# A decoder layer on one core: a tile of their own for the memory's raw weights, and VectorE alone for the low parts of the mixer's value weights

## The chip, the cores and the metric

The kernel runs on one core of a Trainium2 chip. The time is device microseconds of one execution, and a kernel's time is the median of its runs. Five engines work beside each other: TensorE (PE; its weight loads are listed as PEld), VectorE (DVE), ScalarE (ACT), GpSimd (POOL) and SyncE (SP). Here SP does nothing but issue transfers, and POOL issues some too. Each engine takes its instructions strictly in the order in which they were put on it.

## What is computed

One layer, for 512 tokens of a prompt and 64 tokens of samples (576 together), all in float32:

```
u    = rms(x) * g_pre_mix;   proj = u @ w_in            # z, xbc, dt, q, k, v, gates
y_ssd = rms(ssd_scan(...) * silu(z)) * g_ssm_out
h_ml  = rms(mlstm_scan(q, k, v, ...)) * g_mlstm_out * sigmoid(og)
x = x + rms(concat(y_ssd, h_ml) @ w_out) * g_post_mix   # the output projection
mk, mv = (rms(mem) * g_mem) @ w_mem_k,  ... @ w_mem_v   # 256 rows of memory, 4 heads
x = x + rms(cross_attention(rms(x) * g_pre_x, mk, mv) @ w_xo) * g_post_x
x = x + rms(swiglu(rms(x) * g_pre_ffn)) * g_post_ffn
```

What matters below are two of these products: `v`, the mixer's values (part of `u @ w_in`), and the output projection with the preparation of the memory's weights for head 3 beside it.

## The kernel before

Every large product is taken in three matmuls on numbers that are split into a high part (rounded to the matmul's type) and a low part (what is left): high by high, high by low, low by high (L201 to L203; L772 to L774 for the values). Weights come in units of 128 x 1024 numbers, 512 KB. `split_w` (L173) does this for one unit: SP loads it into a `raw` tile (two buffers), ACT rounds it into `whi` (L181), and a low part `wlo` is made from `raw` and `whi` (three buffers each). The next load into a `raw` buffer waits until its last reader is done, and the next `whi` waits until PE has finished with the unit three before it.

The low part is made in one of three ways. `cut` says how many of the 1024 columns VectorE subtracts (L188). For the other columns, with `acc=True`, ACT writes the negated high part into `wlo` (L185), and POOL issues a transfer that adds the raw weights to it from memory (L186); without `acc`, GpSimd subtracts. The mixer's projection (the `win` tiles) and the values (`wv`, eight units, two for each of four heads) use `cut` 512 with `acc=True`.

The values are computed by `gemm_tok` (L753) around 165 to 250 us, in between the chunks of the SSD scan (tiles `lm`, `ps_yi`, `xs`, `h`) and other projections. A scheduler that simulates a timeline sets the order of instructions on every engine, so that these pieces are woven into each other.

The output projection, about 401 to 512 us, runs in two passes over eight output tiles j. The first (`ps_o1`) takes the SSD half. The second (`out2`, L1139, `ps_o2`) takes the mLSTM half; its units are called o0 to o7 here. Each output tile has two halves of tokens, the first of 256 and the second of 320. For j = 0 to 3 the second half and then the first are done together; for j = 4 to 7 first all second halves, then the first halves of 7, 6, 5 and 4, the unit o4 being loaded a second time. Beside each `out2(j)` of j = 0 to 3 stand `presplit` (parts of later weights: loaded by POOL, rounded by ACT into `preh`, subtracted by VectorE and written back by POOL), `memory` (the memory's activations: squares on ACT, sums on VectorE) and `wm_split(j)`.

`wm_split` (L1153) makes the high and low parts of four weight units of the memory's head 3, whole, into `wmh` and `wml`, by `split_w` with `to=`: so the load goes through the same two `raw` buffers as the units of the output projection, ACT rounds (L192) and VectorE subtracts (L193). `wmh` takes the place of `mixs_h`, which the first pass reads to its end. PE first needs `wmh` and `wml` after the output projection, from 512.6 us.

Of the kernel before, what the change touches and what calls it, by code (L numbers as in the profile page):

```python
# [11 lines left out]
F32 = mybir.dt.float32  # L12
# [3 lines left out]
ALU = mybir.AluOpType  # L16
# [3 lines left out]
P = 128  # L20
# [88 lines left out]
CUT = 512  # L109
# [7 lines left out]
def build(nc, tc, ctx, I, O):  # L117
    V, A, G, S, TE = nc.vector, nc.scalar, nc.gpsimd, nc.sync, nc.tensor
# [17 lines left out]
    def GP(name="g"):  # L136
        return pg.tile([P, 512], F32, name=name, tag="g")
# [33 lines left out]
    loads = []  # L171

    def split_w(src, n=1024, cut=CUT, acc=False, pool=None, to=None, raw=None):  # L173
        if raw is None:
            raw = wp.tile([P, 1024], F32, name="raw", tag="raw", bufs=2)
        loads.append(S.dma_start(raw[:, :n], src))
        if to:
            split(*to, raw[:, :n])
            return to
        hi, lo = [(pool or wp).tile([P, 1024], F32R, name=k, tag=k, bufs=NWX if pool else 3) for k in ("whi", "wlo")]  # L180
        A.copy(hi[:, :n], raw[:, :n])  # L181
        for e, a, b in ((V, 0, cut), (G, cut, n)):
            if b > a and e is G and acc:

                A.activation(lo[:, a:b], hi[:, a:b].bitcast(F32), AF.Copy, scale=-1.0)  # L185
                G.dma_start(lo[:, a:b], src[:, a:b], accum_op=ALU.add)  # L186
            elif b > a:
                e.tensor_tensor(lo[:, a:b], raw[:, a:b], hi[:, a:b].bitcast(F32), op=ALU.subtract)  # L188
        return hi, lo

    def split(hi, lo, src, eng=None):
        A.copy(hi, src)  # L192
        (eng or V).tensor_tensor(lo, src, hi.bitcast(F32), op=ALU.subtract)  # L193
# [12 lines left out]
    def gemm2(units, xh, xl, evac, name, halves=(0, 1), alloc=None, order=None, parts=HALVES):  # L206
        for i in halves:
            t0, n = parts[i]
            ps = (alloc or GP)(name)[:, :n]
            m = gemm(ps, units, xh, xl, t0, n, order=order)  # L210
            evac(t0, n, ps)
        return m

    def act(t):
        return lambda k, t0, n: t[:, k, t0:t0 + n]
# [455 lines left out]
    for g in range(2):  # L671
        for hb in range(2):
            dst = cpad[:, g, 4 * hb:4 * hb + 4, :].rearrange("p b t -> p (b t)")
            src = bc[:, 2 + g, TP + 32 * hb:TP + 32 * hb + 32]
# [4 lines left out]
    for g in range(2):  # L679
# [13 lines left out]
        for h in range(8):  # L693
            k, j = h % 2, (8 * g + h) // 2
# [55 lines left out]
        G.memset(v_[:, :, 256:257], 1.0)  # L750
        G.memset(v_[:, :, 257:258], 0.0)

    def gemm_tok(src, xh_, xl_, chunks, evac, acc=False, units=None):  # L753

        units = units or [split_w(src[:, i, :], acc=acc) for i in range(2)]
        for c0 in range(0, len(chunks), 2):
            ps = GP("ps_v")
            for c, (t0, n) in enumerate(chunks[c0:c0 + 2]):
                if n == TS:

                    for k in range(KT):
                        hi, lo = units[k // 4]
                        j = (k % 4) * 256
                        mm(ps[:, 0:256], xh_(k, t0, P), hi[:, j:j + 256], start=k == 0, stop=k == KT - 1, skip_group_check=True)
                        mm(ps[:n, 0:256], xh_(k, t0, n), lo[:, j:j + 256], start=False, stop=k == KT - 1, skip_group_check=True)
                    break
                for k in range(KT):
                    hi, lo = units[k // 4]
                    j = (k % 4) * 256
                    ah, al = xh_(k, t0, n), xl_(k, t0, n)  # L770
                    o = ps[:n, c * 256:c * 256 + 256]
                    mm(o, ah, hi[:, j:j + 256], start=k == 0, stop=False, skip_group_check=True)  # L772
                    mm(o, al, hi[:, j:j + 256], start=False, stop=False, skip_group_check=True)
                    m = mm(o, ah, lo[:, j:j + 256], start=False, stop=k == KT - 1, skip_group_check=True)  # L774
            evac(c0, ps)
        return m
# [12 lines left out]
    for h in range(4):  # L789
        gemm_tok(I["wv"][h], U, UL, CHUNKS, v_evac(h), True)  # L790
# [29 lines left out]
    for h in range(4):  # L820
# [17 lines left out]
        for c in range(4):  # L838
# [3 lines left out]
                        op=ALU.mult)  # L842
# [233 lines left out]
    at = st.enter_context(tc.tile_pool(name="attn", bufs=1, reuse_waits="tile"))  # L1076
# [6 lines left out]
    evs, ahead = [], []  # L1083
# [43 lines left out]
    def memory_norm():  # L1127
        rmem[0] = rstd_cols([ssqm], CHUNKS[:2], "rmem", alloc=B1)
        rstd_rows(rmem[0], CHUNKS[:2], rmem_b, B1)
# [9 lines left out]
    def out2(j, i):  # L1139
        return gemm2([(*weights(("o", j), I["wout"][j, 1], cut=1024), KT)], act(mixm_h), act(mixm_l), o2_evac(j), "ps_o2", [i])  # L1140
# [9 lines left out]
    wmh, wml = SL0("wmh").rearrange("p k t -> p (k t)"), SL(2, "wml", F32R).rearrange("p k t -> p (k t)")  # L1150
    wm = [(wmh[:, 1024 * i:1024 * i + 1024], wml[:, 1024 * i:1024 * i + 1024]) for i in range(4)]

    def wm_split(i):  # L1153
        split_w(I["wmk"][6 + i] if i < 2 else I["wmv"][3][:, i - 2, :], to=wm[i])

    def chain2(i, js):

# [4 lines left out]

    for j in range(4):
        out2(j, 1)
        out2(j, 0)
        presplit(j < 3)
        memory(range(2 * j, 2 * j + 2))
        wm_split(j)
    memory_norm()
    for j in range(4, 8):  # L1170
        out2(j, 1)
# [171 lines left out]
    mk, m = mem_key(3, wm[:2])  # L1343
# [29 lines left out]
    for h in range(3, -1, -1):  # L1373
        xq(2 * h + 1, 0)
        xq(2 * h, 0)
        if last:
            mk = mem_key(h)
# [219 lines left out]
    for n_, (key, p) in enumerate(order):  # L1597
        src = I[{"xo": "wxo", "g": "wgate", "u": "wup"}[key[0]]][key[1]]
# [813 lines left out]
```

## Time and profile before

| What | Value |
|---|---|
| runs (3) | 1118.76 us median, 1115.33 to 1123.21 |
| the profiled execution | 1119.24 us, its span 1117.5 us |
| granted TensorE clock, mean | 0.997 |
| PE busy | 1095.2 us (98%) |
| PE busy, first 16 us / last 18 us of the span | 13.84 us / 10.92 us |
| DVE, ACT, POOL busy | 770.2, 609.5, 225.2 us |
| moved by DMA | 184.44 MB, mean 165 GB/s |

The profile of one execution lists for each instruction its start, its length and, where its engine stood idle before it, what ended that idle time. "PE ps_o L201 <- ACT whi L181: 3.8, 2, 2.0" reads: PE, before writing the tile `ps_o` at line 201, waited for ACT's instruction on `whi` at line 181, 3.8 us in total, 2 times, 2.0 us at most. The view of stages gives for a stretch of time each engine's busy time, the granted clock (1.00 is full), the share of time that the 16 DMA engines were busy, and GB/s. In the timelines a row is start, length, engine, line, operation, written and read tiles, shapes and count.

### The profile page before, as it was taken

To read this page: it belongs to the slowest core of one execution; us is meant where nothing else is said; L and a number is where in the kernel's file an instruction comes from. 1 tells how busy PE (TensorE), PEld (TensorE's weight loads), DVE (VectorE), ACT (ScalarE), POOL (GpSimd) and SP (SyncE) were. 2 spreads that over 40 slices of the span, in tenths; PEclk is the share of its full clock that TensorE was granted. 3 is DMA by queue.
4 is the path that set the end of the run, shared out by engine and by line. 5 is a ranking of instruction groups with operands and counts; after the bars stand their busy time and mean duration, and the time that the engine had idled before them with its cause. 6 is when DMAs were issued, how large, how long until landed. Compare 5 with 4: busy or idle time off the path is not lost.

```text
span 1117.5 us, 21277 instructions
## 1 busy us (share of the span) xinstructions
PE 1095.2 (98%) x8355; PEld 1043.7 (93%) x8355; DVE 770.2 (69%) x1521; ACT 609.5 (55%) x1130; POOL 225.2 (20%) x309
## 2 busy tenths in 40 slices
PE   9999999999999999989999999999999999999997
PEld 8999889798998999989988889999999999999997
DVE  6796775457786785558755455686578878887655
ACT  6867534355563465556534445644465556556654
POOL 1343544323122121110044301100000210020000
PEclk9999999999999999989999999999999999999999
DMA  6785565634564437863487765742552873397432
GB/s 209 171 152 131 132 179 145 177 86 143 143 192 125 122 141 264 279 229 95 152 257 263 250 212 164 233 152 94 165 157 86 186 168 90 83 234 218 101 139 85
DMA packets 60584, 184.44 MB, mean 165 GB/s; under 512 B 6684, under 2 KB 10908, under 8 KB 59972
## 3 DMA queue, kind: packets, MB, share of 16 engines
q1 hardware_dynamic: 44324, 142.19, 39.0%
q0 software_dynamic: 15872, 40.38, 17.1%
q8 instruction: 65, 1.06, 0.4%
q10 hardware_dynamic: 288, 0.52, 0.1%
q14 instruction: 35, 0.29, 0.1%
HBM read 153.75 MB, written 29.30 MB: 164 GB/s over the span
## 4 chain that ended last, share of the span: by engine, by line
PE 82%; DVE 4%; DMA 4%; ACT 3%; issue 2%; DVEq 0%; ACTq 0%; SPq 0%; POOLq 0%
PE ps_in L201 5%; PE ps_in L203 5%; PE ps_in L202 5%; PE ps_g L1725 3%; PE ps_g L1726 3%; PE ps_g L1727 3%; PE ps_u L1726 2%; PE ps_u L1725 2%; PE ps_u L1727 2%; PE ps_o L201 2%; PE ps_o L203 2%; PE ps_o L202 2%; PE ps_dn L201 2%; PE ps_dn L203 2%; PE ps_dn L1932 2%; PE ps_dn L202 2%
## 5 line engine op out<-in xcount | busy, mean ns | idle before, releaser
L201 PE MATMUL ps_in<-uh,whi 128*128 128x320 f32 (+1 forms) x544 | 165.4, 304 | 1.3 <-DVE cb L426 1.1
L203 PE MATMUL ps_in<-uh,wlo 128*128 128x320 f32 (+1 forms) x544 | 163.1, 300 | 0.0
L202 PE MATMUL ps_in<-ul,whi 128*128 128x320 f32 (+1 forms) x544 | 162.2, 298 | 0.0
L181 ACT CAST whi<-raw 128x1024 fp32r<-128x1024 f32 (+1 forms) x102 | 102.9, 1011 | 79.5 <-PE ps_in L202 20.1
L188 DVE TENSOR_TENSOR wlo<-raw,whi 128x512 fp32r<-128x512 f32 (+1 forms) x94 | 86.2, 917 | 60.3 <-ACT whi L181 59.6
L201 PEld LDWEIGHTS ps_in<-uh,whi 128*128 128x128 f32 x544 | 103.0, 189 | 3.9 <-DVE cb L426 1.4
L203 PEld LDWEIGHTS ps_in<-uh,wlo 128*128 128x128 f32 x544 | 102.9, 189 | 1.7 <-issue 1.3
L202 PEld LDWEIGHTS ps_in<-ul,whi 128*128 128x128 f32 x544 | 103.1, 189 | 0.8
L186 POOL DMA_DIRECT2D wlo<-win x32 | 28.3, 884 | 93.6 <-ACT wlo L185 83.3
L1725 PE MATMUL ps_g<-b,whi 128*128 128x288 f32 x144 | 42.7, 297 | 1.2 <-ACT cc L1793 1.0
L201 PE MATMUL ps_o<-mixm_h,whi 128*128 128x256 f32 (+1 forms) x128 | 39.4, 308 | 3.8 <-ACT whi L181 3.8
L1725 PE MATMUL ps_u<-b,whi 128*128 128x288 f32 x144 | 42.8, 297 | 0.0
L1726 PE MATMUL ps_u<-b,whi 128*128 128x288 f32 x144 | 42.5, 295 | 0.0
L1726 PE MATMUL ps_g<-b,whi 128*128 128x288 f32 x144 | 42.5, 295 | 0.0
L202 PE MATMUL ps_o<-mixm_l,whi 128*128 128x256 f32 (+1 forms) x128 | 39.0, 305 | 0.0
L203 PE MATMUL ps_o<-mixm_h,wlo 128*128 128x256 f32 (+1 forms) x128 | 38.7, 306 | 0.0
L201 PE MATMUL ps_xo<-qh,whi 128*128 128x288 f32 x128 | 38.0, 302 | 0.4 <-ACT whi L181 0.3
L201 PE MATMUL ps_xq<-u2h,whi 128*128 128x320 f32 (+1 forms) x128 | 38.2, 303 | 0.0
L202 PE MATMUL ps_xq<-u2l,whi 128*128 128x320 f32 (+1 forms) x128 | 38.0, 298 | 0.0
L203 PE MATMUL ps_xq<-u2h,wlo 128*128 128x320 f32 (+1 forms) x128 | 37.9, 296 | 0.0
L202 PE MATMUL ps_xo<-ql,whi 128*128 128x288 f32 x128 | 37.7, 295 | 0.0
L774 PE MATMUL ps_v<-wlo,uh 128*128 128x256 f32 x128 | 36.7, 290 | 0.9 <-DMA wlo<-wv 0.9
(777 smaller groups left out, 3914.4 us busy)
## 6 DMA issues: line engine op xcount, KB each, us to landing
raw<-win SPq DMA_DIRECT2D x35, 512.0 KB, 3.7
raw<-wout SPq DMA_DIRECT2D x17, 512.0 KB, 4.5
kva<-kc SPq DMA_DIRECT2D x16, 512.0 KB, 7.0
kva<-vc SPq DMA_DIRECT2D x16, 512.0 KB, 7.0
raw<-wxq SPq DMA_DIRECT2D x13, 512.0 KB, 3.7
raw<-wgate SPq DMA_DIRECT2D x13, 512.0 KB, 5.3
raw<-wup SPq DMA_DIRECT2D x13, 512.0 KB, 4.3
wlo<-win POOLq DMA_DIRECT2D x24, 256.0 KB, 5.4
```

The source lines that it names most:

```text
L181: A.copy(hi[:, :n], raw[:, :n])
L186: G.dma_start(lo[:, a:b], src[:, a:b], accum_op=ALU.add)
L188: e.tensor_tensor(lo[:, a:b], raw[:, a:b], hi[:, a:b].bitcast(F32), op=ALU.subtract)
L201: mm(ps, wh, ah, start=i == 0, stop=False)
L202: mm(ps, wh, al, start=False, stop=False)
L203: m = mm(ps, wl, ah, start=False, stop=i == len(tiles) - 1)
L774: m = mm(o, ah, lo[:, j:j + 256], start=False, stop=k == KT - 1, skip_group_check=True)
L1725: mm(ps, wh, b[0][:, k, :], start=start and k == 0, stop=False, skip_group_check=True)
L1726: mm(ps, wh, b[1][:, k, :], start=False, stop=False, skip_group_check=True)
L1727: m = mm(ps, wl, b[0][:, k, :], start=False, stop=k == 3, skip_group_check=True)
L1932: mm(ps, wh, bl, start=False, stop=False, skip_group_check=True)
```

## The change

The first part touches `gemm_tok`. Where it splits its own units, the parameter `acc` now selects `cut`: the values, which pass `True`, get `cut=1024`, so VectorE subtracts all 1024 columns and neither L185 nor L186 is called; the memory's values pass nothing, get `cut=CUT` (512) and stay as they were. The `win` tiles keep their adding transfers.

The second part replaces `wm_split` by two functions. `wm_load(j)` loads the memory's unit into a tile `wmr` of its own. This tile has one buffer, in the place of `mk`, which is written only later. The load is issued behind the latest `raw` load, and `wm_load` stands between the second and the first half of `out2(j)`. `wm_split(j)` then rounds on ACT, behind the latest evacuation of the output projection, and subtracts on VectorE.

```diff
-    def gemm_tok(src, xh_, xl_, chunks, evac, acc=False, units=None):
+    def gemm_tok(src, xh_, xl_, chunks, evac, acc=None, units=None):
 
-        units = units or [split_w(src[:, i, :], acc=acc) for i in range(2)]
+        units = units or [split_w(src[:, i, :], cut=CUT if acc is None else 1024) for i in range(2)]
...
-    def wm_split(i):
-        split_w(I["wmk"][6 + i] if i < 2 else I["wmv"][3][:, i - 2, :], to=wm[i])
+    def wm_load(i):
+        t_ = at.tile([P, 1024], F32, name="wmr", tag="mk", bufs=1)
+        with tc.issue_after(loads[-1].ins):
+            S.dma_start(t_, I["wmk"][6 + i] if i < 2 else I["wmv"][3][:, i - 2, :])
+        return t_
+
+    def wm_split(i, t_):
+        hi, lo = wm[i]
+        with tc.issue_after(evs[-1].ins):
+            A.copy(hi, t_)
+        V.tensor_tensor(lo, t_, hi.bitcast(F32), op=ALU.subtract)
...
     for j in range(4):
         out2(j, 1)
+        wm_raw = wm_load(j)
         out2(j, 0)
         presplit(j < 3)
         memory(range(2 * j, 2 * j + 2))
-        wm_split(j)
+        wm_split(j, wm_raw)
```

The scheduler moves instructions of other lines too, between about 140 us and 500 us. Three places matter for the steps below.

SP's queue in the second pass of the output projection, before. The rows named `wout` are the units o1 to o7, in order; `wmk` and `wmv` are the memory's units 0 to 3.

```order
L176 DMA raw_5520<-wmk 128x1024
L176 DMA raw_5524<-wout 128x1024
L176 DMA raw_5606<-wmk 128x1024
L176 DMA raw_5610<-wout 128x1024
L176 DMA raw_5692<-wmv 128x1024
L176 DMA raw_5696<-wout 128x1024
L176 DMA raw_5776<-wmv 128x1024
L176 DMA raw_5796<-wout 128x1024
L176 DMA raw_5832<-wout 128x1024
L176 DMA raw_5868<-wout 128x1024
L176 DMA raw_5904<-wout 128x1024
```

And after, where o1 to o7 are the seven `wout` rows from `raw_5508` to `raw_5888`:

```order
L1156 DMA wmr_5462<-wmk 128x1024
L176 DMA raw_5508<-wout 128x1024
L176 DMA raw_5594<-wout 128x1024
L176 DMA raw_5680<-wout 128x1024
L176 DMA raw_5780<-wout 128x1024
L176 DMA raw_5816<-wout 128x1024
L1156 DMA wmr_5544<-wmk 128x1024
L176 DMA raw_5852<-wout 128x1024
L1156 DMA wmr_5630<-wmv 128x1024
L176 DMA raw_5888<-wout 128x1024
L1156 DMA wmr_5716<-wmv 128x1024
```

Five units of the output projection now follow each other, and the memory's units 1 to 3 come later, each between two of them.

ACT's queue in the same place, before: the rounding of the memory's unit 3, and then those of o4 (`whi_5798`) and o5 (`whi_5834`).

```order
L192 CAST wmh_5442<-raw_5776 128x1024
L266 ACTIVATE sq_5642<-f_mix_4903 128x320
L1136 ACTIVATE f_mix_4903<-f_mix_4903,par_77 128x320
L266 ACTIVATE sq_5672<-f_mix_4903 128x256
L266 ACTIVATE sq_5684<-memraw_4909 128x256
L1136 ACTIVATE f_mix_4903<-f_mix_4903,par_77 128x256
L1091 CAST preh_5676<-prel_5594 128x1024
L181 CAST whi_5798<-raw_5796 128x1024
L266 ACTIVATE sq_5689<-memraw_4909 128x256
L181 CAST whi_5834<-raw_5832 128x1024
```

And after: the memory's units 2 (`wmr_5630`) and 3 (`wmr_5716`), with o6 (`whi_5854`) and o7 (`whi_5890`).

```order
L1162 CAST wmh_5426<-wmr_5630 128x1024
L266 ACTIVATE sq_5675<-memraw_4893 128x256
L266 ACTIVATE sq_5712<-f_mix_4887 128x320
L1136 ACTIVATE f_mix_4887<-f_mix_4887,par_77 128x320
L181 CAST whi_5854<-raw_5852 128x1024
L266 ACTIVATE sq_5744<-f_mix_4887 128x256
L266 ACTIVATE sq_5754<-memraw_4893 128x256
L1136 ACTIVATE f_mix_4887<-f_mix_4887,par_77 128x256
L1091 CAST preh_5748<-prel_5666 128x512
L266 ACTIVATE sq_5759<-memraw_4893 128x256
L1162 CAST wmh_5426<-wmr_5716 128x1024
L181 CAST whi_5890<-raw_5888 128x1024
```

o4 stood behind the memory's last unit before; now o4 stands ahead of the memory's unit 1, o6 behind its unit 2, and o7 right behind its unit 3.

POOL's queue while the values are computed, as a difference (`h` and `xs` belong to the SSD scan):

```order
 L722 TENSOR_TENSOR h_1896<-h_1896,decs 128x1024
-L631 TENSOR_TENSOR xs<-xs,ec 128x384
-L186 DMA wlo<-wv 128x512
-L631 TENSOR_TENSOR xs<-xs,ec 128x384
-L186 DMA wlo<-wv 128x512
+L631 TENSOR_TENSOR xs<-xs,ec 128x384 x2
 L722 TENSOR_TENSOR h_1925<-h_1925,decs 128x1024
 L722 TENSOR_TENSOR h_1924<-h_1924,decs 128x1024
-L186 DMA wlo<-wv 128x512
```

The adding transfers of the values are gone from POOL, here three of the eight; the subtractions that replace them are rows of VectorE that grow from 512 to 1024 columns.

## The prediction, made before the result was known

> **What bounds the kernel now.** I read the page first, then what PE waited for, then the stages around its longest wait, then PE's own timeline there, then the chain that ended last.
>
> ```profile
> span 1117.5 us, 21277 instructions
> PE 1095.2 (98%) x8355; PEld 1043.7 (93%) x8355; DVE 770.2 (69%) x1521; ACT 609.5 (55%) x1130; POOL 225.2 (20%) x309
> ...
> PE ps_o L201 <- ACT whi L181: 3.8, 2, 2.0
> PE ps_nh L911 <- DMA c<-c: 1.7, 1, 1.7
> PE ps_hs L715 <- DMA h<-h: 1.5, 1, 1.5
> ...
> PE ps_v L774 <- DMA wlo<-wv: 0.9, 2, 0.7
> ```
>
> PE is the bound: it is idle for only 22.3 of 1117.5 us. The edit removes no PE work, so it can earn only idle time, and time at a low granted clock. The largest wait of all (3.8 us) is at the output projection for a unit's high part. Two smaller ones, `ps_hs` and `ps_v`, stand where the values are computed.
>
> ```profile
> 470.00:474.00 4.00, 4.00 (x33) 4.00 (x32) 0.95 (x1) 0.00 (x0) 0.00 (x0) 1.00 0.95 335
> 474.00:478.00 4.00, 4.00 (x33) 4.00 (x32) 2.21 (x4) 2.69 (x6) 1.08 (x2) 1.00 0.33 90
> 478.00:481.00 3.00, 0.89 (x5) 0.42 (x3) 2.52 (x5) 2.62 (x5) 0.09 (x1) 1.00 0.88 295
> 481.00:484.00 3.00, 1.27 (x5) 1.27 (x6) 2.71 (x5) 2.31 (x5) 0.46 (x1) 0.62 0.66 210
> 484.00:487.00 3.00, 3.00 (x13) 3.00 (x13) 1.70 (x4) 2.67 (x5) 0.54 (x1) 0.50 0.91 313
> 487.00:490.00 3.00, 3.00 (x18) 3.00 (x17) 0.83 (x3) 0.25 (x1) 0.00 (x0) 0.74 0.88 261
> ```
>
> Columns: stretch, its length, busy time of PE, PEld, DVE, ACT, POOL, granted clock, DMA share, GB/s. PE falls to 0.89 of 3 us, and then the clock falls to half: the hole goes on costing while PE is "busy" again.
>
> ```profile
> 474.06 0.31 PE L203 MATMUL ps_o<-mixm_h,wlo 128*128 128x320 f32 x1
> 475.23 0.31 PE L202 MATMUL ps_o<-mixm_l,whi 128*128 128x320 f32 x1
> ...
> 477.92 0.28 PE L202 MATMUL ps_o<-mixm_l,whi 128*128 128x256 f32 x1
> 478.04 0.28 PE L203 MATMUL ps_o<-mixm_h,wlo 128*128 128x256 f32 x1
> 480.36 0.42 PE L201 MATMUL ps_o<-mixm_h,whi 128*128 128x320 f32 x1 [2.03 <-ACT whi L181]
> ...
> 482.73 0.63 PE L201 MATMUL ps_o<-mixm_h,whi 128*128 128x320 f32 x1 [1.81 <-ACT whi L181]
> ...
> 490.00 0.31 PE L201 MATMUL ps_o<-mixm_h,whi 128*128 128x320 f32 x1
> ```
>
> At full clock eight 320-column matmuls are 1.17 us, so 0.146 each, and a 256-column one is 0.12. Unit o4 was due at 478.16. From 480.36 to 490.00 PE issues 34 matmuls, 34 x 0.146 = 5.0 us of work in 490.00 - 478.16 = 11.84. **The hole costs 6.8 us**: 3.8 of waiting, 3.0 of low clock.
>
> ```profile
> 458.10 4.70 DMA raw<-wmv
> ...
> 465.47 8.73 DMA raw<-wmv
> 474.23 1.06 ACT wmh L192
> 475.31 1.24 DVE wml L193
> 476.56 4.99 DMA raw<-wout
> 481.63 1.05 ACT whi L181
> 482.73 0.63 PE ps_o L201
> ```
>
> The chain says why: the load of the memory's unit 3 took 8.73 us in one of two `raw` buffers. ACT and VectorE had to use it up before o5 could be loaded into that buffer, at 476.56. Between 474 and 478 the transfers were nearly idle (0.33, 90 GB/s) while weights were wanted: a buffer was missing, not bandwidth.
>
> **Part 1, a tile for the raw memory weights.** Loads, roundings and subtractions stay four each. What goes is the turn in `raw`: o1 to o5 load one behind another, each when the unit two before it is split. o4 is rounded when PE leaves o1 (465.4 by the 6.4 us of 24 x 0.146 + 24 x 0.12), o5 when it leaves o2 (471.8); they are due at 478.16 and 481.7. Both waits of the trace go.
>
> What is late next? The new tile has one buffer, so the memory's units form a chain: load, round (1.06), subtract (1.24), next load, with some 0.3 for the handovers. In ACT's order o6 stands behind unit 2 and o7 right behind unit 3; whoever waits for that load holds them. I time it from these rows:
>
> ```profile
> 459.62 0.42 ACT L262 ACTIVATE ssqo<-f_mix 128x256 f32<-128x256 f32 x1 [1.58 <-DVE f_mix L1134]
> 460.49 1.03 ACT L1091 CAST preh<-prel 128x1024 fp32r<-128x1024 f32 x1
> 461.55 1.22 DVE L1092 TENSOR_TENSOR prel<-prel,preh 128x1024 f32<-128x1024 f32 x1 [1.96 <-ACT preh L1091]
> 462.69 0.48 DVE L1134 TENSOR_TENSOR f_mix<-f_mix,ps_o 128x320 f32<-128x320 f32 x1
> ```
>
> PE leaves o0 at 459.0, which frees o3's `whi`. ACT then does o3 (1.05), two pieces of `f_mix` (about 0.9), `preh` (1.03) and unit 0 by 463.2. VectorE, behind `prel` and `f_mix`, ends its subtraction at about 465.1. With a load of L us each, unit 3 is rounded, o7 after it, and o7's low part made, at 465.1 + 3L + 2 x 2.6 + 1.1 + 1.05 + 1.2 = 473.6 + 3L. PE is due at o7 at 478.16 + 3 x 3.5 = 488.7 and needs that low part at its third matmul, at 489.1. So o7 is late by 3L - 15.5. The same count for o6, behind unit 2 and 1.4 us of `f_mix` and squares, gives 472.5 + 2L, 483.7 at an L of 5.6 and due at 485.5, so o6 is in time. Only the unit length of the load is unknown: the rows give 4.70, 4.99 and 8.73, so the lateness is 0 to 10.7 us. I take L = 5.6, between the median and the mean of the three: late by 1.3. **The hole then costs 1.3 in place of 6.8, a gain of 5.5**; the bounds are a gain of 6.8 and a loss of 10.7 + 3.0 (low clock as before) - 6.8 = 6.9. SP's queue behind these loads holds o6, o7, the second o4 and `x`, none of them due before 485.
>
> A single stall of 1.3 us should not bring the low clock: the windows show it only behind two stalls near 2 us within 5. The Trainium skill's page "TensorE: Matmul & The Clock Gate", section "What's actually happening", says that the clock halves after an idle window of about 3.4 us and needs about as long of busy time to come back. The trace agrees with the first half (3.8 us idle around two matmuls) and shows the low clock for longer, in three windows from 481 to 490. By that rule the 1.3 us cost their bare length, so the sum stays as it is.
>
> **Part 2, the values' low parts.** Removed: eight POOL issues with eight adding transfers of 256 KB, and eight ACT pieces of 0.63. Added: 512 columns in each of eight subtractions.
>
> ```profile
> L188 DVE TENSOR_TENSOR wlo<-raw,whi 128x512 fp32r<-128x512 f32 x14 | 10.3, 738 | 7.5 <-ACT whi L181 7.4
> L185 ACT ACTIVATE wlo<-whi 128x512 fp32r<-128x512 f32 x14 | 8.6, 628 | 0.2
> L186 POOL DMA_DIRECT2D wlo<-wv x8 | 7.0, 915 | 20.6 <-ACT wlo L185 20.6
> ...
> 190.06 1.27 SPq L176 DMA_DIRECT2D raw<-wv  x2
> 191.63 8.82 DMA o_ssms<-h
> 200.51 3.50 DMA h<-h
> ...
> 232.57 6.40 DMA wlo<-wv
> ```
>
> A low part was ready 6.4 us after POOL's issue; VectorE needs 1.24 for all 1024 columns. So `ps_v`'s 0.9 us goes. `ps_hs` waited 1.5 us for a load of `h` that had to wait for a store of 8.82 us; beside that store ran two raw loads (1 MB) and two adding transfers (0.5 MB). Without the latter it moves 1.5 of 2.0 MB, about 6.6 us, so the load starts 2.2 us sooner: gain 0 to 1.5, I take 1.2, as bandwidth was shared with more than these.
>
> The cost: 1.24 - 0.74 (the mean of 14) = 0.50 us in each of eight places, 4.0 us of VectorE. If every one delayed a PE that waits for `lm` or a PSUM evacuation, that would be 4.0 us; if none, 0. PE shows no wait for VectorE's `lm` in that stage, so I take 0.5.
>
> POOL can lengthen such a subtraction:
>
> ```profile
> 131.85 1.27 DVE L188 TENSOR_TENSOR wlo<-raw,whi 128x512 fp32r<-128x512 f32 x1 [0.44 <-ACT whi L181]
> 163.15 1.86 DVE L612 TENSOR_TENSOR lm<-lm,cbs 128x512 f32<-128x512 f32 x1
> 162.52 4.28 POOL L722 TENSOR_TENSOR h<-h,decs 128x1024 f32<-128x1024 f32 x2 [0.48 <-PE ps_hs L715]
> ```
>
> The subtraction that is 0.74 in the mean took 1.27 in one place, and another 512-column row 1.86 while POOL worked on `h`: up to 1.1 us more for each collision. The page "SBUF — State Buffer" of the Trainium skill, section "SBUF: two separate sides", says that a VectorE instruction with two inputs in SBUF and a GpSimd instruction exclude each other for their whole length, while transfers use other ports; by that rule moving the addition from transfers to VectorE invites just this. The trace agrees, with 1.86 for 0.74.
>
> **Everything else.** The scheduler's order differs from 140 to 500 us. The wait of `ps_nh` (1.7) lies there; its load still follows a store in SP's queue. I give the new order 0, with 1.7 either way.
>
> **The sum**, against the profiled execution's 1119.24: - 5.5 (hole) - 0.9 (`ps_v`) - 1.2 (`ps_hs`) + 0.5 (VectorE) = - 7.1, so 1112.1 us. That execution lies 0.5 above the median of the three runs, within their spread, so I leave it there.
>
> **Rivals.** *The one-buffer chain* (it ends slower). If the memory's loads take 8.73, as the last did, o7 is 10.7 late and the clock falls: + 6.9 - 1.6 (the values' three terms) = 1124.5. For it: that row, and 313 GB/s in this stretch. Against: the other two rows, and that this slow load shared its time with loads that now come earlier. It decides from 3L - 15.5 + 3.0 > 6.8 + 1.6, L above 7.0. *Bandwidth binds anyway*: the same bytes cross between 460 and 490 us at up to 335 GB/s, so the hole only moves and only the values' 1.6 stay: 1117.6. For it: DMA shares of 0.9; against: 0.33 between 474 and 478, just ahead of the hole. *VectorE late among the values*: every subtraction delays PE, 4.0 for my 0.5: 1115.6, and 8 x 1.1 = 8.8 us more if each also collides with POOL. Against: no PE wait on VectorE there.
>
> **How the numbers follow.** Forecast 0.62 (own range 1108 to 1116), chain 0.15, bandwidth 0.15, VectorE 0.08. The best case is all terms at their best end, - 6.8 - 0.9 - 1.5 - 1.7 = 1108.3; less a run's spread, 1106.5. Above, 1119 takes in the bandwidth case and the mild half of the chain. One per cent, 11.2 us, is about what a measurement of this kernel can tell from no change. Faster by more needs better than every best end together: 0.10. Slower by more needs the chain at its worst and the collisions: 0.04. Within: 0.86.
>
> **What would show it.** Right: no PE wait for `whi` at 478, the clock at 1.00 there, o7's rounding behind unit 3's with PE idle about 1 us at 489; no `ps_v` wait for a transfer; `ps_hs` short. Wrong in part 1: a hole of several us at o6 or o7 with a `wmr` load ahead of it, or the old hole in place. Wrong in part 2: PE idle behind VectorE's `wlo` or `lm`, or subtractions of 2 us and more. A time above 1119 or below 1106.5 would say that the reordering, which I set at zero, decided.

## The result and the profile after

The changed kernel takes 1113.54 us (median of 20 runs, 1110.66 to 1117.88), the kernel before 1118.26 (20 runs, 1112.47 to 1123.62). The ratio is 0.9954 with a 95% interval of 0.9939 to 0.9970, so 5.1 us less; the prediction was 1112.1. The execution profiled after is the shortest of its 20, and the one before lay near its median, so the two profiles differ by 8.6 us in span, more than the medians do.

The page and PE's waits of the changed kernel:

```profile
span 1108.9 us, 21249 instructions
PE 1093.2 (99%) x8355; PEld 1041.6 (94%) x8355; DVE 772.8 (70%) x1521; ACT 605.1 (55%) x1122; POOL 217.2 (20%) x301
...
PE ps_nh L911 <- DMA c<-c: 1.7, 1, 1.7
...
PE ps_o L201 <- DVE tmp L991: 0.5, 1, 0.5
...
PE ps_rb L251 <- DVE rmem_r L240: 0.2, 1, 0.2
```

The waits of `ps_o` for `whi` (3.8), of `ps_hs` (1.5) and of `ps_v` (0.9) are gone, that of `ps_nh` stands as it was, and two small ones are new: 0.5 near the start of the output projection (at 402.78 us, 3.5 us behind its first matmul), 0.2 for the memory's norm. The stages that had the hole, in the view by stage (the same stretches and columns as in the prediction):

```profile
474.00:478.00 4.00, 4.00 (x34) 4.00 (x33) 2.21 (x3) 2.72 (x4) 1.62 (x3) 1.00 0.72 229
478.00:481.00 3.00, 3.00 (x22) 3.00 (x21) 3.00 (x6) 2.82 (x7) 0.00 (x0) 1.00 0.90 328
481.00:484.00 3.00, 3.00 (x24) 3.00 (x23) 1.85 (x5) 0.92 (x3) 0.54 (x1) 1.00 1.03 293
484.00:487.00 3.00, 3.00 (x22) 3.00 (x22) 2.15 (x2) 2.71 (x4) 0.15 (x1) 1.00 0.90 288
487.00:490.00 3.00, 2.75 (x20) 2.52 (x19) 2.36 (x9) 1.10 (x3) 0.71 (x1) 1.00 1.01 420
```

PE is nearly full and the clock stays at 1.00. Over the whole hole, 460 to 490 us, the transfers move more than before, not less: 290 GB/s for 254. The chain that ended last now runs through the new tile:

```profile
463.16 5.06 DMA wmr<-wmk
468.25 1.06 ACT wmh L1162
469.33 1.24 DVE wml L1163
470.58 5.73 DMA wmr<-wmv
476.33 1.06 ACT wmh L1162
477.45 0.66 issue
478.67 5.08 DMA wmr<-wmv
483.77 1.06 ACT wmh L1162
484.89 1.11 issue
485.99 1.22 DVE wlo L188
```

This is the one-buffer chain of the prediction: load, round, subtract, next load. The loads take 5.06 to 5.73 us, and the last row is o7's low part, ready at 487.21. PE asks for it at 487.48, so the chain ends 0.3 us before it would cost anything.

To compare executions I use one more measure: from PE's first matmul of the output projection (here 399.31) to its last (504.47). It holds the same matmuls in every kernel, so what differs is idle time, clock and how other work is woven in. These are all the profiles of this study, in us:

| Kernel | projection begins | lasts | from its end to the span's end |
|---|---|---|---|
| before; a second profile | 401.61; 402.74 | 110.95; 108.88 | 604.9; 605.0 |
| no memory loads | 401.50 | 103.96 | 604.9 |
| tile alone; a second profile | 401.87; 401.47 | 110.59; 104.89 | 606.8; 606.1 |
| values' part alone; a second | 401.53; 398.98 | 105.30; 107.26 | 606.7; 606.5 |
| the change; a second profile | 399.31; 399.72 | 105.16; 106.68 | 604.4; 605.7 |
| change with two tiles; a second | 398.70; 399.92 | 104.72; 104.71 | 605.3; 607.3 |
| change, wide loads | 400.23 | 109.51 | 608.0 |
| GpSimd for half of the values | 403.32 | 110.52 | 605.3 |
| two tiles, `win` by VectorE too | 404.34 | 109.71 | 604.7 |

### The profile page after: what moved, and what is told of

Read it like the earlier page. It is cut to its first block, busy times and chain, and to the rows that moved or that the text cites. A ratio compares the mean times of both kernels' runs of the same rounds, so it can differ in the third digit from the quotient of the medians.

```text
span 1108.9 us, 21249 instructions
## 1 busy us (share of the span) xinstructions
PE 1093.2 (99%) x8355; PEld 1041.6 (94%) x8355; DVE 772.8 (70%) x1521; ACT 605.1 (55%) x1122; POOL 217.2 (20%) x301
## 4 chain that ended last, share of the span: by engine, by line
PE 82%; DVE 5%; ACT 4%; DMA 4%; issue 1%; POOL 0%; DVEq 0%; ACTq 0%; SPq 0%; POOLq 0%
PE ps_in L201 5%; PE ps_in L202 5%; PE ps_in L203 5%; PE ps_g L1735 3%; PE ps_g L1736 3%; PE ps_g L1737 3%; PE ps_u L1735 2%; PE ps_u L1736 2%; PE ps_u L1737 2%; PE ps_o L201 2%; PE ps_o L203 2%; PE ps_o L202 2%; PE ps_dn L201 2%; PE ps_dn L203 2%; PE ps_dn L1942 2%; PE ps_dn L202 2%
## 5 line engine op out<-in xcount | busy, mean ns | idle before, releaser
L188 DVE TENSOR_TENSOR wlo<-raw,whi 128x512 fp32r<-128x512 f32 (+1 forms) x94 | 90.4, 963 | 55.8 <-ACT whi L181 55.1
L186 POOL DMA_DIRECT2D wlo<-win x32 | 28.0, 885 | 87.5 <-ACT wlo L185 71.5
L201 PE MATMUL ps_o<-mixs_h,whi 128*128 128x320 f32 (+1 forms) x128 | 38.2, 298 | 0.5 <-DVE tmp L991 0.5
L202 PE MATMUL ps_o<-mixs_l,whi 128*128 128x320 f32 (+1 forms) x128 | 37.7, 294 | 0.0
```

Of the source, the lines that this page charges most:

```text
L201: mm(ps, wh, ah, start=i == 0, stop=False)
L202: mm(ps, wh, al, start=False, stop=False)
```

## The experiments

The theory to test: a `raw` buffer was missing, and its own tile closes the hole; the values' part is a smaller gain of its own. The rivals: the new order brought it, bandwidth binds, or the one-buffer chain takes back what was won.

**Each part alone.** The tile alone is the kernel before with the second half of the diff; the values' part alone is this one line of it:

```diff
-        units = units or [split_w(src[:, i, :], acc=acc) for i in range(2)]
+        units = units or [split_w(src[:, i, :], cut=CUT if acc is None else 1024) for i in range(2)]
```

> The kernel before with the second part alone: the memory's raw weights in a tile of their own, the values' low parts as before. My theory: the hole at the output projection is a missing raw buffer, so it closes here in full (6.8 us of waiting and low clock; in the profile after, stretch 460 to 490, PE 29.75 of 30 at a clock of 1.00), while the waits of ps_v (0.9) and ps_hs (1.5) stay. Time 5 to 7 us below before, 1111.3 to 1113.3. Rival, the new order of the stages from 140 us on brought the gain, or the values did: within 1.5 us of before, about 1117 to 1118. Second rival, bandwidth: the wait for whi moves to another unit of the output projection and stays above 2 us.

> The kernel before with the first part alone: VectorE subtracts all 1024 columns of the values' units, the memory's weights go through the raw buffers as before. My theory: 0.9 (ps_v) and 0 to 1.5 (ps_hs) are won and 0.5 is paid to VectorE, 1.6 us in all, so 1116 to 1117.5, with the hole of about 6.8 us and the low clock still there at about 478 to 490. Rival, the values' part does most of what the change did: 1113 to 1114. Rival, VectorE becomes late among the values: 0 to 4 us slower than before, 1118 to 1122, with PE waiting for wlo or lm between 165 and 250 us.

Measured: the tile alone 1116.19 us, ratio 0.9971 (0.9947 to 0.9994); the values' part alone 1115.45, ratio 0.9965 (0.9951 to 0.9980). The tile gave less than I expected and the values more. The profiles were stranger still. With the values alone the hole was nearly gone, though the memory's weights still went through `raw`; with the tile alone there was one. Its rows, from the chain that ended last and from PE's timeline:

```profile
469.23 7.94 DMA wmr<-wmk
...
479.52 4.67 DMA wmr<-wmv
...
490.49 0.58 PE L226 MATMUL ps_ss<-c,ssqm 128*128 128x1 f32 x4 [2.59 <-DVE ssqm L267]
```

The load of the memory's unit 1 took 7.94 us, everything behind it came late, and PE waited 2.59 us for a sum over the memory's squares, which stand behind the memory's rounding in ACT's queue. That execution took 1121.10 us, the longest of its 12. So one profile of a kernel didn't say what the kernel does, and the next runs were second profiles.

**Is the hole the kernel's, or one execution's?** Three kernels again, unchanged, and one that leaves out the four loads (it computes the memory's head 3 from other numbers):

```diff
-        split_w(I["wmk"][6 + i] if i < 2 else I["wmv"][3][:, i - 2, :], to=wm[i])
+        split(*wm[i], memraw[:, 0:4, :].rearrange("p a b -> p (a b)"))
```

> The kernel before, unchanged, for a second profile and against itself. What is open: with the values' part alone the profile showed the output projection closed (29.69 of 30 us in 460 to 490) though the memory's weights still went through the raw buffers. Theory A, the hole belongs to the kernel before: PE again loses 5 to 8 us between 470 and 492 (waits for whi and a low clock). Theory B, the hole belongs to one execution, in which one load took 8.73 us: with a load near 5.5 us PE loses less than 2 us there, and the median of the runs contains only part of the 6.8 us that the prediction took from one profile. Ratio to itself 0.998 to 1.002 by either.

> The changed kernel, unchanged, for a second profile and beside the others on one chip. By both theories the output projection stays closed or loses up to 2 us (o7's low part was 0.3 us early in the first profile, so a memory load 1 us longer than 5.3 us costs up to 3 us by the one-buffer chain), and the time is 4 to 6 us below before, 1113 to 1115.

> The kernel with the values' part alone, a second time. Theory A, the values' part closes the hole for a reason of its own (the order it gives, or the traffic it takes away ahead): PE again loses under 1 us between 460 and 490, and the time stays at 3.5 to 4.5 us below before. Theory B, the hole comes and goes with the length of the memory's loads: in another execution PE may lose up to 7 us there, and the values' part is worth what its own stage gives, 1.3 to 2.1 us between 190 and 250 us, so that the time falls to 1.5 to 3 us below before when both results are taken together.

> The kernel before without the four loads of the memory's head 3 in the output projection; the rounding and the subtraction work on activations that are there already, so head 3 of the memory is computed from the wrong numbers. This takes away every wait for these loads, in every execution, and 2 MB of traffic, and leaves the values as they were. Theory A, the hole of 6.8 us is in most executions: 6 to 7.5 us below before, ratio 0.9935 to 0.995. Theory B, it is in some executions and smaller in others: 2 to 4.5 us below before, ratio 0.996 to 0.998, and what the tile can bring at most is that much.

Measured, as ratios to the kernel before: itself 1.0011 (0.9986 to 1.0035); the change 0.9968 (0.9953 to 0.9984); the values' part alone 0.9990 (0.9971 to 1.0009); without the loads 0.9956 (0.9938 to 0.9973), which is 4.9 us of 1117.80, within 3.0 to 6.9. The 0.9956 lies between the two theories (0.9935 to 0.995 and 0.996 to 0.998). The hole is in the kernel before in both profiles, but its size is the execution's. PE's waits for o4 and o5 in the second profile of before, with the last memory load ahead of them:

```profile
467.26 7.48 DMA raw<-wmv
474.77 1.06 ACT wmh L192
...
480.90 0.41 PE L201 MATMUL ps_o<-mixm_h,whi 128*128 128x320 f32 x1 [1.45 <-ACT whi L181]
482.88 0.55 PE L201 MATMUL ps_o<-mixm_h,whi 128*128 128x320 f32 x1 [1.42 <-ACT whi L181]
```

And the same in the two profiles of the values' part alone. In the first, o4 does not wait and the row is o5's; the second has both:

```profile
479.61 0.42 PE L201 MATMUL ps_o<-mixm_h,whi 128*128 128x320 f32 x1 [0.31 <-ACT whi L181]
```

```profile
477.21 0.42 PE L201 MATMUL ps_o<-mixm_h,whi 128*128 128x320 f32 x1 [0.75 <-ACT whi L181]
...
479.02 0.41 PE L201 MATMUL ps_o<-mixm_h,whi 128*128 128x320 f32 x1 [1.25 <-ACT whi L181]
```

Take the start of o4's first matmul less its wait as the time when o4 was due, and look at how far ahead of it ACT begins `wmh` of unit 3, that is, when unit 3 has landed (with the values alone o4's first matmul is at 478.84):

| Profile | last memory load, us | landed ahead of o4's due time | waits of o4 and o5 |
|---|---|---|---|
| before | 8.73 | 4.10 | 3.84 |
| before, again | 7.48 | 4.68 | 2.87 |
| GpSimd for half | 7.99 | 4.84 | 2.52 |
| values alone, again | 7.32 | 5.39 | 2.00 |
| values alone | 5.85 | 6.84 | 0.31 |

The later the load lands, the longer the wait, in every row. Between it and o4 stand, in ACT's order, `wmh`, squares, `f_mix`, `preh` and then o4's rounding, and o5's load waits for the buffer. So the hole has two causes, one for each wait. In the first four rows it is 5.0 us from the start of `wmh` to that of o4's rounding, which takes 1.05 itself: o4 is ready 6.1 us behind the landing, and 6.1 less the third column gives waits of 2.0, 1.4, 1.3 and 0.7, as measured (2.03, 1.45, 1.29, 0.75). O4's own weights were there by then. In the kernel before:

```profile
raw<-wout SPq DMA_DIRECT2D x1, 512.0 KB, 5.7
...
470.98 0.33 SPq L176 DMA_DIRECT2D raw<-wout  x1
...
479.26 1.04 ACT L181 CAST whi<-raw 128x1024 fp32r<-128x1024 f32 x1
```

Issued at 470.98 and landed 5.7 us later, they waited 2.6 us for ACT (1.5 to 2.6 in the four profiles). Rounded on landing, o4 would have been in time in all four. O4's wait is thus ACT's order, and only o5's, whose load is issued behind unit 3's subtraction, is the missing buffer that the prediction read from the chain. The tile comes with a new order, and together they take away both. The order alone, or a third `raw` buffer alone, was not tried.

**The tile alone, again, and two tiles.** The second is the change with this:

```diff
-        t_ = at.tile([P, 1024], F32, name="wmr", tag="mk", bufs=1)
+        t_ = at.tile([P, 1024], F32, name="wmr", tag=("mk", "wm2")[i % 2], bufs=1)
```

> The tile alone, a second time. The output projection, from PE's first matmul of it to its last, took 110.95 and 108.88 us in two profiles of the kernel before, 103.96 without the memory's loads, 105.16 and 106.68 with the whole change, and 110.59 with the tile alone, in an execution whose 1121.1 us is the longest of its 12. My theory: the tile alone closes most of it, and that one execution had three of the presplit's transfers of 9.31, 6.97 and 10.56 us ahead, which made the first memory rounding 6 us later than in the changed kernel (466.31 for 460.25), and a memory load of 7.94 us. So a second profile shows 104.5 to 107.5 us, and both timings together lie 3 to 5 us below before. Rival: without the values' part the tile doesn't help, the projection takes 109 us or more again, and the time is within 2 us of before.

> The change with two tiles for the memory's raw weights, used in turn, so the loads no longer wait for the subtraction just before. In the profile after, the chain that ended last runs through these loads (5.06, 5.73, 5.08 us) but o7's low part is ready at 487.2, 0.3 us before PE asks for it. My theory: the one-buffer chain costs nothing at this length of load, so this kernel equals the changed one within 1 us, 1112.5 to 1114.5, with o7 rounded 4 us or more earlier. Rival, the chain still costs: 1 to 3 us faster than the changed kernel, 1110.5 to 1112.5.

> The change with two tiles for the memory's raw weights, a second time, since the first timing has 6 runs only. Theory 1, the one-buffer chain costs where a load is long (0.7 us with 5.3 us loads in the second profile of the change, as a wait of ps_rb; 2.7 in all against the projection without loads): the two tiles make the time 1 to 2 us shorter than the change, 5.5 to 7 us below before, and the projection takes 104 to 105.5 us. Theory 2, it costs nothing in most executions: 4 to 5.5 us below before, as the change.

Measured: the tile alone 1116.99 us, 0.9984 (0.9957 to 1.0010), and its projection lasted 104.89, so it does close it when its loads are short (4.46, 5.48 and 4.68 us in that chain). My reason for the first profile held only in part: the presplit's transfers were long here too (9.27, 7.01 and 8.00 us), and only the first memory load was not. The two timings taken together give about 2.5 us, less than the 3 to 5 I expected.

Two tiles took 1111.93 us, 0.9940 (0.9916 to 0.9963), and 1111.67 us, 0.9923 (0.9896 to 0.9950), with 6 runs each. My expectation, that a second tile brings nothing, was wrong: the change's medians are 1113.54 and 1113.91, so the one-buffer chain costs about 1.9 us in a typical execution, and the first profile of the change, with 0.3 us to spare, was a good one. The size is rough: by the ratios to the kernel before it is 3.3 us, the two kernels were not timed beside each other, and the intervals overlap. In the second profile of the change the chain did end last:

```profile
489.21 0.42 PE L203 MATMUL ps_o<-mixm_h,wlo 128*128 128x320 f32 x1 [0.21 <-DVE wlo L188]
491.59 0.40 PE L251 MATMUL ps_rb<-c,rmem_r 128*128 128x128 f32 x2 [0.78 <-DVE rmem_r L240]
```

PE waits 0.21 us for o7's low part and 0.78 for the memory's norm. With two tiles neither wait is there, and the stage is full (first profile):

```profile
460.00:490.00 30.00, 30.00 (x222) 29.99 (x220) 23.37 (x41) 21.40 (x37) 4.96 (x10) 1.00 0.81 285
```

**A longer load in the one buffer.** The change, with this, and with o6 and o7 held behind the memory's units 2 and 3 in ACT's order as in the change:

```diff
-        t_ = at.tile([P, 1024], F32, name="wmr", tag="mk", bufs=1)
+        t_ = at.tile([P, 2, 1024], F32, name="wmr", tag="mk", bufs=1)
         with tc.issue_after(loads[-1].ins):
-            S.dma_start(t_, I["wmk"][6 + i] if i < 2 else I["wmv"][3][:, i - 2, :])
+            S.dma_start(t_, I["wmk"][5 + i:7 + i].rearrange("a p n -> p a n") if i < 2 else I["wmv"][3])
```

> The change with a load of twice the width for each of the four memory units (1 MB in place of 512 KB into a wider tile, still one buffer; half of it isn't used), and with o6 and o7 held behind the memory's units 2 and 3 in ACT's order as they are in the changed kernel. My theory: the one-buffer chain has a break point. With loads of 5.3 us o7's low part was 0.3 us early; each load now takes 9 to 11 us by twice the bytes at the rate seen, so it comes 3 x 4.7 = 14 us later (11 to 17), and the low clock behind such a stall adds about 3 us: 1125 to 1134, with PE's wait at o6 or o7 for whi or wlo of 8 us and more in all. Rival, the chain isn't what sets o6 and o7, only the bytes count: 2 MB more at the 290 GB/s of the stretch are at most 7 us, and PE loses less than that: 1113.5 to 1120.

Measured: 1118.28 us, 0.9984 (0.9962 to 1.0007), some 4.5 us above the change by the medians and 2.6 by the ratios, and the projection lasted 109.51. The time fell into the rival's range, but the profile shows my mechanism: the three loads of the chain, then PE's waits at o7.

```profile
465.00 5.36 DMA wmr<-wmk
...
472.71 6.32 DMA wmr<-wmv
...
481.38 7.32 DMA wmr<-wmv
...
490.77 0.41 PE L205 MATMUL ps_o<-mixm_h,whi 128*128 128x320 f32 x1 [2.06 <-ACT whi L185]
492.22 0.41 PE L207 MATMUL ps_o<-mixm_h,wlo 128*128 128x320 f32 x1 [0.66 <-DVE wlo L192]
```

What I mis-sized was the load. Twice the bytes made it 1.0 us longer (mean 6.33 for 5.29), not 4.7. Three times 1.0 less the 0.3 to spare is 2.8 us of lateness; PE waits 2.06 + 0.66 = 2.72. That this fits so well is partly chance: the chain also began 1.8 us later than in the change's first profile (465.00 for 463.16), and PE came to o7 1.5 us later (488.71 for 487.18). The Trainium skill's page "DMA: Bandwidth & Descriptors", section "Anatomy of one DMA — SWDGE (gpsimd) path", gives for that path a fixed part of about 2.0 us and 436 GB/s; an estimate from it for 512 KB more is 1.2 us. These loads go by SP's queue, not by that path, but the 1.0 us is near it, and I could have used it in place of the rate of the stretch.

**What in the values' part pays.** The kernel before, where GpSimd subtracts the second half of the columns: no adding transfers, and VectorE as before.

```diff
-        units = units or [split_w(src[:, i, :], acc=acc) for i in range(2)]
+        units = units or [split_w(src[:, i, :]) for i in range(2)]
```

> The kernel before, with the second half of each of the values' low parts subtracted by GpSimd in place of the adding transfers; VectorE keeps its first half. It tells the removed transfers from the work that moved to VectorE. In the profiles the output projection begins at 401.5 to 402.7 us with the adding transfers and at 398.7 to 400.2 (one at 401.5) without, 2.2 us earlier in the mean. Theory 1, the transfers cost this (their 6.4 us until the low part is ready, and the bandwidth beside the store that holds h): it begins at 399 to 401 here too, no wait of ps_v for a transfer, and the time is 1 to 3 us below before. Theory 2, that VectorE does it is what counts, since GpSimd takes 1.74 us for each of the eight and is in use for h and xs there: 401.5 us or later, a wait of ps_v for GpSimd, and the time within 1 us of before or slower.

Measured: 1118.86 us, 0.9991 (0.9972 to 1.0011); the projection begins at 403.32. The second theory is right in its time, but `ps_v` does not wait for GpSimd, as it expected; and the first is right in one thing, that `ps_v` waits for no transfer any more. POOL's row, SP's store of `h`, and PE's wait:

```profile
190.81 3.49 POOL L188 TENSOR_TENSOR wlo<-raw,whi 128x512 fp32r<-128x512 f32 x2 [0.89 <-ACT whi L181]
...
194.75 0.38 SPq L728 DMA_DIRECT2D o_ssms<-h  x1
...
205.42 1.07 PE L715 MATMUL ps_hs<-h,cpad 128*32 128x512 f32 x8 [2.12 <-DMA h<-h]
```

The store starts at 194.75 here, at 191.63 to 192.27 with adding transfers (five profiles, mean 191.9) and at 192.44 to 192.95 with VectorE (seven, mean 192.7). So the store comes 0.8 us later with VectorE and 2.9 with GpSimd, where `ps_hs` waits 2.12. Part of this was there before the two subtractions just ahead: VectorE's `xdt` near 186 us is already 0.5 and 1.7 us later, and from it to the store it takes 5.51 us with adding transfers, 5.84 with VectorE and 6.72 with GpSimd.

**More of the same.** Two tiles, and the `win` units with `cut` 512 whole by VectorE as well:

```diff
-                w = split_w(I["win"][i], cut=cut, acc=True)
+                w = split_w(I["win"][i], cut=cut and 1024, acc=True)
```

> The change with two tiles for the memory's raw weights, and with the win units that were shared between VectorE and adding transfers (those with 512 columns each) whole by VectorE as well. If the adding transfers cost among the values because they are late and take bandwidth, they cost less here, where no wait of PE for a win low part is in the profile: by my theory 0 to 1.5 us better than two tiles alone, 5.5 to 8 us below before. Rival: VectorE, which gets some 0.5 us in each of 24 places, becomes late between 250 and 400 us, where it is at 77 percent already: 1 to 6 us slower than two tiles alone, with PE waiting for wlo or for an evacuation by VectorE there.

Measured: 1123.11 us, 1.0019 (0.9999 to 1.0038); that is 11.4 us above two tiles alone by the medians, beyond even my rival's 1 to 6. The projection begins at 404.34:

```profile
404.34 0.38 PE L201 MATMUL ps_o<-mixs_h,whi 128*128 128x256 f32 x1 [4.05 <-ACT mixs_h L192]
405.71 1.97 PE L866 MATMUL ps_ht<-c,num 128*128 128x128 f32 x8 [0.99 <-DVE num L862]
```

PE waits 4.05 us for the first operand of the projection and 0.99 for VectorE. The row of the long wait names ACT, and ACT's own rows say why, first here and then with two tiles alone (second profile):

```profile
400.91 2.56 ACT L1006 ACTIVATE mixm_h<-qk,ghalf 128x512 fp32r<-128x512 f32 x4
403.62 2.96 ACT L192 CAST mixs_h<-xs 128x576 fp32r<-128x576 f32 x5
```

```profile
394.80 4.69 ACT L192 CAST mixs_h<-xs 128x576 fp32r<-128x576 f32 x8
401.30 3.18 ACT L1006 ACTIVATE mixm_h<-qk,ghalf 128x512 fp32r<-128x512 f32 x5
```

Here `mixs_h`, which PE needs first, stands behind `mixm_h`; with two tiles alone it stands ahead. So the nearest cause is the order that the scheduler chose. My rival's mechanism is not what the profile shows: from 250 to 400 us PE is busy all 150.0 us, and VectorE 116.2 us, for 115.1 with two tiles alone. VectorE is late in one place far ahead, where PE waits 2.33 us for it at 51 us (1.1 and 1.2 in the two profiles of two tiles). Whether the longer subtractions would cost anything in the old order was not tried.

## Why the prediction was right, point by point

**The total** was 1.4 us off the median (1112.1 for 1113.54) and inside the range; the direction and the kinds of gain were right. That it came out so near is partly luck: the gain was 5.1 us for 7.1, the sum started from an execution 1.0 us above the later median of before, and the parts were shared out differently. By two timings each, the tile alone gave 2.5 us for the 5.5 of the hole and the values' part alone 2.5 for 1.6.

**The hole, 6.8 us: half of the mechanism, and one execution's size.** The step that read a kernel's cost from a single profile failed. In that profile the projection was 110.95 - 103.96 = 7.0 us longer than without the loads, in the second 108.88 - 103.96 = 4.9, and the timing without the loads gives 4.9. The two sizes follow from the waits and from what the runs showed of the clock (last section): each fall of the clock costs 1.7 us. The first profile had 3.84 of waits and two falls, 7.2; the second 2.87 and one, 4.6. "Not bandwidth" holds: the changed stretch moved 290 GB/s for 254 between 460 and 490 us and PE was nearly full. The bandwidth rival falls. "A buffer was missing" holds for o5 only (1.81 of the 3.84 us); o4's 2.03 were its place in ACT's queue, which the prediction did not tell apart. It also had o5 due at 481.7; PE takes o5's first matmul two behind o4's first, so it was due at 480.92.

**The one-buffer chain, o7 late by 1.3 us: right mechanism, smaller lateness at o7.** Predicted loads of 5.6 us, measured 5.06, 5.73 and 5.08; with their mean of 5.29 the prediction's 3L - 15.5 gives 0.4 late, and o7's low part was 0.3 early in the first profile and 0.2 late in the second. In the profiles of the change the projection is 1.2 and 2.7 us above the one without loads, of which 0.5 is the new wait near its start; a second tile gives about 1.9 back. In the second profile the wait is at o7's `wlo`, where it was looked for, and more at `ps_rb`, which the prediction had not named: the memory's squares stand behind the same loads in ACT's queue. As a rival (slower than before, from loads of 7 us) the chain didn't come true; the wide loads, at a mean of 6.33, brought the time near that of before.

**`ps_v`, 0.9: right.** 0.7 to 0.9 in five profiles with adding transfers, none in those without.

**`ps_hs`, 1.2: 0.85, for two reasons where I had one.** The wait is 1.2 to 1.6 us with adding transfers (mean 1.4) and 0 to 1.0 with VectorE (seven profiles, mean 0.5). From the issue of the store to that of `h`'s load it took 7.3 us in the mean (five profiles), now 6.2 (seven): that was the argued half. But as the store itself starts 0.8 us later, the load of `h` is issued only 0.2 us sooner (198.9 for 199.1 in the mean), where the prediction had 2.2. Most of the gain is that the load itself got shorter, from 4.7 to 3.5 in the mean, and the change's rows offer a reason:

```profile
192.64 0.34 SPq L728 DMA_DIRECT2D o_ssms<-h  x1
198.49 0.33 SPq L711 DMA_DIRECT2D h<-h  x1
201.07 7.97 SPq L728 DMA_DIRECT2D o_ssms<-h  x2
```

The next store is issued 2.6 us behind this load (1.8 to 2.8 in the seven profiles); with adding transfers it was 0.4 us behind (200.89 after 200.51), so the two ran beside each other. What makes it later is VectorE, which ends its part of `h` later. So the cost that I booked may have paid a part of itself back; this is a reading, and the first profile of before, where the load took 3.50 beside that store, doesn't bear it out.

**VectorE, 0.5: not shown as a cost of its own.** Its 1024 columns took 1.22 to 1.25 us, 2.36 for two in a row, with no wait of PE for them among the values. The one new wait for VectorE is the 0.5 for `tmp` near the projection's start; it is in all seven profiles with VectorE and in the one with GpSimd, so the longer rows alone do not explain it. The collisions with GpSimd did not come among these eight. They are real, though: with GpSimd at the other half, VectorE's 512 columns took 1.45 us beside it in place of 0.69.

**The new order, 0: about right where I looked, not behind it.** The projection begins 2.1 us earlier in the mean (401.84 in five profiles with adding transfers, 399.77 in seven with VectorE) where the values' terms said 1.6. But from its end on, the faster kernels lose 1.2 us in the mean: 606.1 in the eight profiles with the tile, the values' part, the change or two tiles, for 604.9 to 605.0. Those profiles show waits of `ps_sa` or `ps_os` for a cache tile (up to 1.3 us, 0.5 before) and of `ps_ss` for `ssqxo` (0.6 to 1.6, none before) that come and go. I had no term for a gain that is given back behind its stage. The cause stays open. That PE now comes earlier than the loads does not explain it: without the memory's loads PE left the projection at 505.46, 7.1 us earlier than before, and the rest still took 604.9, while in the first profile of the tile alone it left at 512.46, as before, and the rest took 606.8.

**Open.** The values' part alone had a short projection twice (105.30 and 107.26), with the same order there as before. Its last memory load was shorter (5.85 and 7.32 us for 8.73 and 7.48), and why is not known; its two timings (0.9965 and 0.9990) leave room for chance. Taken together the two parts' timings give 2.5 us each, and the change's two 4.4, which fits within their intervals.

## What to carry to other kernels

A wait behind a transfer has a spread, not a size: look at the same load in several executions, or take the load away and time the kernel, before you book its whole length as a gain. A tile of its own takes a load out of another's buffers, but with one buffer it makes a chain, and everything queued behind that chain's rounding in an in-order engine is late with it, so a second buffer was worth some 2 us more here. And a wait behind a buffer can hold two waits: ask of each weight whether it is missing, or there and not yet reached in its engine's queue. Moving work to an engine that has room in the mean is not safe by that alone: VectorE took the values' halves for next to nothing, but the kernel in which it also took the `win` halves was 11 us slower, most visibly where the new order put the projection's first operand late.

## What the runs showed of the hardware that I had not expected

**The clock falls after less idle time than I thought, and in equal portions.** A single wait of 2.12 us at `ps_hs` was followed by a fall, in the kernel with GpSimd at half of the values (the view by stage):

```profile
202.00:204.00 2.00, 1.30 (x11) 1.09 (x10) 0.00 (x0) 0.00 (x0) 0.73 (x1) 1.00 0.86 135
204.00:206.00 2.00, 0.58 (x8) 0.16 (x8) 0.00 (x0) 0.00 (x0) 0.00 (x0) 1.00 0.94 377
206.00:208.00 2.00, 2.00 (x15) 1.49 (x8) 0.69 (x1) 0.00 (x0) 1.42 (x1) 0.67 0.05 16
208.00:210.00 2.00, 2.00 (x9) 1.48 (x8) 0.00 (x0) 0.00 (x0) 2.00 (x2) 0.50 0.00 0
```

The time at half clock is (1 - 0.67) x 2 / 0.5 = 1.3, then 2.0, and 0.1 in the next stretch (0.98): 3.4 us, which costs 1.7 us. The kernel with wide loads had 0.67, 0.50 and 0.97 in three stretches of 2 us behind its waits of 2.72, again 3.4 us. The second profile of before had 0.83 and 0.60 in two stretches of 3 us, 3.4 us once more, and the first, as the prediction shows it, 0.62, 0.50 and 0.74: 2.3 + 3.0 + 1.6 = 6.8, twice 3.4. Falls of 3.4 us also came behind single waits of 1.84 (`ps_nh`, values alone) and 1.12 us (`ps_ss` for `ssqxo`, wide loads).

The length of the wait does not decide. Two waits of 0.75 and 1.25 us within 3 us left the clock at 1.00, and so did the 1.5 us of the kernel before at `ps_hs` and a wait of 2.33 us at 51 us in the kernel with `win` by VectorE. The same place in two executions, the second profile of before and the first of the tile alone:

```profile
358.90 0.64 PE L911 MATMUL ps_nh<-c,qpad 128*32 128x257 f32 x8 [1.78 <-DMA c<-c]
```

```profile
359.56 0.64 PE L911 MATMUL ps_nh<-c,qpad 128*32 128x257 f32 x8 [1.82 <-DMA c<-c]
```

Behind the first the clock was 0.53 and 0.62 in the two stretches of 2 us from 360; behind the second it stayed at 1.00. The matmuls after these short waits are small (128*32, or one column), so what counts as idle is open too. The Trainium skill's page "TensorE: Matmul & The Clock Gate", section "What's actually happening", has about 3.4 us both for the idle window that halves the clock and for the busy time that brings it back. The second agrees with every fall here; for the first, waits of 1.1 to 2.1 us were enough in some places and 2.3 was not in another, and the measurement decides. So in the prediction "3.0 of low clock" was two portions of 1.7, and its step that a single stall of 1.3 us does not bring the low clock is not safe: a stall of 1 to 2 us may cost 1.7 us on top or nothing.

**A load's length differs from execution to execution.** The memory's loads of 512 KB took 3.6 to 10.7 us, the longest being the first of the four in the new tile (9.0 to 10.7 with one buffer, issued near 430 us, long before its rounding). What sets the length was not isolated. The spread of the kernel's own time was smaller with more buffers, which fits: 1112.47 to 1123.62 before, 1110.66 to 1117.88 with the change (20 runs each), 1110.52 to 1115.74 with two tiles (12 runs).
